# RWKV's triangular inverse by columns, experts' up projections in 512 + 512 + 384 columns, and a longer yield in the routing step

## The chip, the cores and the metric

The program runs on one core of a Trainium2 chip. The metric is the device time of one execution in microseconds (us). The engines are TensorE (PE; its weight loads are PEld), VectorE (DVE), ScalarE (ACT), GpSimd (POOL) and SyncE (SP, which here only starts loads).

## The reference

Two decoder layers over x of 512 tokens by 1024, in float32. Each layer mixes four branches of width 256 and then runs a feed-forward block, dense in the first layer and 2 of 8 experts in the second:

```
for l in range(2):
    h = rmsnorm(x)
    p_rw, p_sb, p_ret, p_conv = split(h @ w_in[l])          # 1024 -> 3328
    y = rwkv7(p_rw), stick_breaking(p_sb), retention(p_ret), conformer_conv(p_conv)
    x = x + (sum_i sigmoid(h @ w_gate[l, i]) * (y[i] @ w_branch[l, i])) @ w_out[l]
    h = rmsnorm(x)
    x = x + (swiglu(h, d_ff=2816) if l == 0 else top2_of_8_experts(h, d_ff=1408))

# rwkv7, per head: state = state * w + (state @ -kk) (x) (kk * a) + v (x) k ;  y = state @ r
# expert: (silu(h @ w1) * (h @ w3)) @ w2, gated by the softmax of the two chosen logits
```

## The kernel before

**Matmuls.** Activations lie with features on partitions and 512 tokens along the row. A product in full precision is three matmuls on a split of each operand into a high and a low part (`split`: ACT copies the high part, DVE subtracts to get the low one). In the mixers the weights come from DRAM through SP into `wraw`, and are split into `whi` and `wlo` of 512 columns; six split buffers of each run ahead of PE. Groups of 24 such matmuls (8 blocks of K, three passes; PSUM tag `mm`) form the weight stream of a layer: first the input projection in the order of `SEQ` (rwkv, retention, conv, stick-breaking), then per branch eight gate groups and eight branch groups, in the order retention, conv, rwkv, stick-breaking, then `w_out`.

**The order of the work.** The four mixers are Python generators that run beside the weight stream. The builder itself keeps a clock of each engine (`Clock`, with its own costs), and at each `slot()` between pieces of the stream it steps a generator when its results should be there (`pump`, `step`). `yield` means that the next step waits until the last is modelled to be finished; `yield NOW` lets it follow at the next slot; `yield 5000.0` waits 5000 ns more of the modelled PE time. So what each engine executes, and in what order, is fixed at build time by these costs; at run time every engine goes through its own list in order. All DVE, ACT and POOL instructions of helpers are recorded on line L213, matmuls on L473, transposes on L477, DMAs on L349, table loads on L370.

**RWKV's substitution.** RWKV works on 8 chunks of 64 tokens for 4 heads. Per chunk and head a unit lower triangular 64 x 64 matrix is inverted, as two 32 x 32 diagonal blocks and a product. All 64 diagonal blocks lie one to a partition: `L` is the strict triangle, `X` the inverse being made, `tmp` a buffer. Row t of X is the sum over earlier rows s of L[s, t] X[s]: one product over t x t elements, and one reduction over s, for t = 1 to 31. Afterwards X goes through DRAM (`d2`, `d3`, on POOL's queue) into `T11` and `TT`, and 32 x 32 matmuls form the rest.

**Stick-breaking chunks** (`sb_chunk`): scores on PE (`mx` buffers, three of them), a chain of exponentials, logarithms and scans on ACT and DVE, transposes back (L477), and a product into `po`.

**Experts.** Experts are sorted by load; ranks 0 to 3 have 192 rows, 4 to 7 have 128, and they run in the order 0, 4, 1, 5, ... The 64 overflow rows of the large ones cost two more matmuls per block (`po<-...`). Here the tokens are the stationary operand (`hh`, `hl`, and `ho` for overflow rows) and the weights stream: each unit of weights is loaded to `mraw`, split to `mhi` and `mlo`, and used. The up projections w1 and w3 go in column ranges `FQ`, the down projection in ranges of K, `FB`; `MRAW` and `MSPL` are the numbers of raw and split buffers. `turn` transposes a finished range of the hidden activations. `moe_prep` prepares the next expert: a one-hot table `O` (`moe_O`), slot tables and the gather (`moe_slots`), then, after `yield 20000.0`, transposes.

Of the kernel before, what the change touches and what calls it, by code (L numbers as in the profile page):

```python
# [19 lines left out]
KC = D // 128  # L20
# [10 lines left out]
N_IN = 3328  # L31
CAP = [192] * 4 + [128] * 4
NREST = 3
MRAW, MSPL = 6, 5
PORD = [0, 4, 1, 5, 2, 6, 3, 7]
NROW = S + 192
ARENA = 34
# [281 lines left out]
class Trunk:  # L319
# [188 lines left out]
    def rwkv(self, out):  # L508
# [154 lines left out]
        TT = m(Q, 64)  # L663
        g.memset(TT[:], 0.0)
        yield
        for t in range(1, 32):
            v.tensor_tensor(tmp[0:64, 0:t, 0:t], X[0:64, 0:t, 0:t].rearrange("p s c -> p c s"),
                            L[0:64, 0:t, t].unsqueeze(1).to_broadcast([64, t, t]), op=OP.mult)
            v.tensor_reduce(X[0:64, t, 0:t], tmp[0:64, 0:t, 0:t], axis=AX.X, op=OP.add)
            if t % 4 == 0 or t > 22:  # L670
                yield NOW
        L.free()
        v.tensor_copy(tmp[0:64], X[0:64].rearrange("p t c -> p c t"))
# [1076 lines left out]
                self.tr(ps[:, k - k0, :], src[0:m, k * 128:(k + 1) * 128], self.c("ident")[0:m, 0:m])  # L1750
            self.split(hi[:, k0:k1, :], lo[:, k0:k1, :], ps[:, 0:k1 - k0, :])

    FQ = [(0, 3), (3, 6), (6, 9), (9, 11)]
    FB = [(0, 3), (3, 6), (6, 9), (9, 11)]

    def moe_units(self, e):

        one = lambda w, a, b: w[bass.ds(e, 1), :, a:b].rearrange("o p f -> p (o f)")
        u = []
        for f0, f1 in self.FQ:  # L1760
            n = (f1 - f0) * 512
            for w in ("moe_w1", "moe_w3"):
                for o in (f0 * 1024, f0 * 1024 + n):
                    u.append((one(self.ins[w], o, o + n), n))
        for f0, f1 in self.FB:
            for d in range(2):
                o = d * (DFE // 128) * 512
                u.append((one(self.ins["moe_w2"], o + f0 * 512, o + f1 * 512), (f1 - f0) * 512))
        return u

    def m_load(self, n):
        while self.nld < min(n, len(self.units)):
            src, cols = self.units[self.nld]
            raw = self.wp.tile([128, 1536], F, name="mraw", tag="mraw", bufs=MRAW)
            self.turn(raw, "mraw", MRAW)
            self.load(raw[:, 0:cols], src, "sp")
            self.raws[self.nld] = raw
            self.nld += 1

    def m_split(self, n):  # L1780
        while self.nsp < min(n, len(self.units)):
            self.m_load(self.nsp + 1)
            cols = self.units[self.nsp][1]
            raw = self.raws.pop(self.nsp)
            t = [self.turn(self.wp.tile([128, 1536], R, name=x, tag=x, bufs=MSPL), x, MSPL) for x in ("mhi", "mlo")]
            self.split(t[0][:, 0:cols], t[1][:, 0:cols], raw[:, 0:cols])
            self.wts[self.nsp] = t
            self.nsp += 1
# [59 lines left out]
    def moe_prep(self, p, put):  # L1848

        slots = []  # L1850
        O = self.moe_O(self.moe_new, self.rkp[:, :, p], CAP[p])
        yield
        self.moe_slots(self.moe_new, O, self.V[:, :, p, :], CAP[p], slots)
        yield 20000.0
        H = [self.mt(n, [128, KC, 128], R, 2) for n in ("hh", "hl")]
        for k0 in (0, 4):
            self.moe_T(slots[0][2][:, k0 * 128:], 4, 128, H[0][:, k0:], H[1][:, k0:])
            yield
        if len(slots) > 1:
            o = self.mt("ho", [128, KC, 128], R, 2)  # L1860
            for k0 in (0, 4):
                self.moe_T(slots[1][2][:, k0 * 128:], 4, 64, o[:, k0:, 0:64], o[:, k0:, 64:128])
                yield
            H.append(o)
        put.append((slots, H))

    def moe_expert(self, slots, H, fill):
# [18 lines left out]
        def unit(blocks, ps, po, x, cols, first, last):  # L1886
            wt = self.m_weight()
            for i, k in enumerate(blocks):
                sl = slice(i * cols, (i + 1) * cols)
                self.stream(ps, po, (x[0][:, k, :], x[1][:, k, :]), x[2][:, k, :] if ov else None,  # L1890
                            (wt[0][:, sl], wt[1][:, sl]), first and i == 0, last and i == len(blocks) - 1)
                if i == 1 and len(blocks) > 2:
                    self.slot()

        for q, (f0, f1) in enumerate(self.FQ):
            n = (f1 - f0) * 128
            gm = self.mt("gm", [128, 384], bufs=2)[:, 0:n]
            go = self.mt("gmo", [64, 384], bufs=2)[:, 0:n] if ov else None
            for j in range(2):
                ps, po = self.ps("mm")[:, 0:n], self.ps("po")[:, 0:n] if ov else None  # L1900
                for h in range(2):
                    unit(range(4 * h, 4 * h + 4), ps, po, H, n, h == 0, h == 1)
                    if h == 0:
                        self.slot()

                def ev(j=j, ps=ps, po=po, gm=gm, go=go, n=n):
# [19 lines left out]
        for i, (f0, f1) in enumerate(self.FB):  # L1926
            for d, (ps, po) in enumerate(acc):
# [5 lines left out]
                            self.v.tensor_scalar(y[1][0:64, sl], self.fold(po, 512), w(1, 64), None, op0=OP.mult)  # L1933
                    self.pending.append(ev)
                self.slot()
                if d and i == 1:
                    for f in todo:
                        f()
                    todo.clear()
# [39 lines left out]
    def moe_rest(self):  # L1979
# [5 lines left out]
        def block(e, rk, V):  # L1985
# [8 lines left out]

            def weights():
                src, n = next(units)
                raw, hi, lo = tile_("rraw", [128, 1536]), tile_("rhi", [128, 1536], R), tile_("rlo", [128, 1536], R)
                nc.sync.dma_start(raw[:, 0:n], src)
                self.split(hi[:, 0:n], lo[:, 0:n], raw[:, 0:n])
                return hi, lo  # L2000
# [9 lines left out]
            for f0, f1 in self.FQ:  # L2010
                n, sl = (f1 - f0) * 128, slice(f0 * 128, f1 * 128)
                pr = [self.ps("mm")[:, 0:n] for _ in range(2)]
                for ps in pr:
                    for h in range(2):
                        unit(range(4 * h, 4 * h + 4), ps, x, n, h == 0, h == 1)
                self.a(gm[:, sl], pr[0], AF.Silu, scale=v[:, 2:3])
                self.v.scalar_tensor_tensor(gm[:, sl], pr[1], v[:, 2:3], gm[:, sl], op0=OP.mult, op1=OP.mult)
            self.moe_T(gm, nf, 128, g[0], g[1])
# [96 lines left out]
```

## Time and profile before

| | us |
|---|---|
| median of 3 runs (1970.99 to 1974.13) | 1971.04 |
| the profiled execution, its own time | 1968.11 |
| its span in the trace | 1966.2 |
| PE busy, share of the span | 1920.0 (98%) |
| DVE busy | 1310.9 (67%) |
| ACT busy | 975.9 (50%) |
| mixers of the first layer (to the dense block) | 8 to 405 |
| dense block | 405 to 920 |
| mixers of the second layer and output projection | 920 to 1405 |
| experts | 1426.7 to 1957.2 |

The stages follow each other in one execution. In the profile a row of the waits names who waited, who ended the wait, the total, the count and the longest. A row of the timeline gives start, duration, engine, line, operation, out<-in by the program's names, the shape and, in brackets, the idle time ahead of it. Durations of matmuls overlap, so their cost is read from one start to the next. A granted clock of 1.00 is TensorE at full speed.

### The profile page before, as it was taken

How to read it: one execution, taken by the hardware profiler on the slowest of the kernel's cores; microseconds unless marked ns; L12 is line 12 of the kernel's file. 1: busy time of each engine (PE TensorE's matmuls, PEld its weight loads, DVE VectorE, ACT ScalarE, POOL GpSimd, SP SyncE). 2: the span in 40 equal slices, each digit the busy share in tenths (PEclk: the TensorE clock that was granted, in tenths of full speed). 3: DMA queues.
4: the chain of work that ended last, by engine and by line, in shares of the span. 5: the costliest groups of instructions: out<-in, count | busy, mean ns of one | idle time of the engine just before them, and what ended most of it. 6: DMA issues, size and time to landing. Idle time of an engine off the chain costs nothing.

```text
span 1966.2 us, 26705 instructions
## 1 busy us (share of the span) xinstructions
PE 1920.0 (98%) x10172; PEld 1583.7 (81%) x10172; DVE 1310.9 (67%) x1970; ACT 975.9 (50%) x1429; POOL 123.7 (6%) x179
## 2 busy tenths in 40 slices
PE   8999899899999999999999999999999999999998
PEld 6778677688888888888778776778898998989987
DVE  6779986555653333356789976546477867768666
ACT  5643354743532232345453345644356756657665
POOL 1001100000000000000110100010101101001000
PEclk9999999999999999999999999999999999999999
DMA  5322311133333233243322322152377968969866
GB/s 190 104 76 76 99 59 64 59 118 99 99 108 97 97 97 97 91 131 125 97 65 81 94 68 71 59 166 92 137 268 246 361 215 293 331 216 330 280 220 215
DMA packets 74677, 284.54 MB, mean 145 GB/s; under 512 B 9536, under 2 KB 11200, under 8 KB 74544
## 3 DMA queue, kind: packets, MB, share of 16 engines
q1 hardware_dynamic: 65088, 254.04, 38.1%
q0 software_dynamic: 9312, 28.73, 5.3%
q8 instruction: 82, 1.34, 0.3%
q14 instruction: 51, 0.42, 0.1%
q10 hardware_dynamic: 144, 0.02, 0.0%
HBM read 266.23 MB, written 14.42 MB: 143 GB/s over the span
## 4 chain that ended last, share of the span: by engine, by line
PE 87%; DVE 6%; ACT 3%; issue 2%; DMA 1%; POOL 0%; SPq 0%; POOLq 0%; DVEq 0%; ACTq 0%
PE mm L473 67%; PE po L473 10%; PE mx L473 8%; DVE s L213 4%; ACT s L213 2%; PE mx L477 2%; DVE wlo L213 1%; DMA out_d<-y,si 1%; ACT whi L213 0%; DVE mlo L213 0%; DMA wraw<-w_gate_d 0%; DMA f<-xt_d 0%; ACT L370 0%; DVE uv L213 0%; ACT mhi L213 0%
## 5 line engine op out<-in xcount | busy, mean ns | idle before, releaser
L473 PE MATMUL mm<-s,whi 128*128 128x512 f32 x3168 | 1006.6, 399 | 20.7 <-DVE s L213 13.1
L473 PEld LDWEIGHTS mm<-s,whi 128*128 128x128 f32 x3168 | 591.2, 189 | 162.8 <-DVE s L213 18.1
L473 PE MATMUL mm<-s,wlo 128*128 128x512 f32 x1584 | 622.6, 393 | 2.2 <-DVE wlo L213 2.0
L213 ACT ACTIVATE whi<-wraw 128x512 fp32r<-128x512 f32 (+1 forms) x432 | 261.0, 620 | 243.4 <-PE mm L473 119.0
L213 DVE TENSOR_TENSOR wlo<-wraw,whi 128x512 fp32r<-128x512 f32 (+1 forms) x432 | 286.8, 680 | 124.2 <-ACT whi L213 123.3
L473 PEld LDWEIGHTS mm<-s,wlo 128*128 128x128 f32 x1584 | 299.8, 189 | 69.7 <-DVE wlo L213 5.9
L213 DVE TENSOR_TENSOR mlo<-mraw,mhi 128x1536 fp32r<-128x1536 f32 (+1 forms) x192 | 307.5, 1620 | 68.4 <-ACT mhi L213 67.8
L213 ACT ACTIVATE mhi<-mraw 128x1536 fp32r<-128x1536 f32 (+1 forms) x192 | 262.2, 1379 | 87.6 <-PE po L473 37.9
L213 DVE TENSOR_TENSOR s<-s,s 128x512 f32<-128x512 f32 (+15 forms) x306 | 222.2, 735 | 40.6 <-ACT s L213 32.5
L213 ACT ACTIVATE s<-s 128x512 f32<-128x512 f32 (+4 forms) x236 | 148.8, 658 | 187.8 <-DVE s L213 182.2
L473 PE MATMUL mm<-mhi,hh 128*128 128x384 f32 (+1 forms) x512 | 169.5, 331 | 0.0
L473 PE MATMUL mm<-mhi,hl 128*128 128x384 f32 (+1 forms) x512 | 165.5, 323 | 0.0
L473 PE MATMUL mm<-mlo,hh 128*128 128x384 f32 (+1 forms) x512 | 165.0, 322 | 0.3 <-DVE mlo L213 0.3
L213 ACT ACTIVATE s<-mm 128x512 f32<-128x512 f32 x108 | 64.1, 594 | 193.9 <-PE mm L473 193.9
L213 DVE TENSOR_TENSOR s<-s,mm 128x512 f32<-128x512 f32 x91 | 62.2, 685 | 136.4 <-PE mm L473 114.6
L473 PEld LDWEIGHTS mm<-mhi,hh 128*128 128x128 f32 x512 | 96.4, 188 | 2.3
L473 PEld LDWEIGHTS mm<-mlo,hh 128*128 128x128 f32 x512 | 96.4, 188 | 1.0 <-DVE mlo L213 1.0
L473 PEld LDWEIGHTS mm<-mhi,hl 128*128 128x128 f32 x512 | 96.5, 189 | 0.3
L473 PE MATMUL po<-mhi,ho 128*128 128x384 f32 (+1 forms) x256 | 83.3, 326 | 0.0
L473 PE MATMUL po<-mlo,ho 128*64 128x384 f32 (+1 forms) x256 | 82.3, 322 | 0.0
L213 DVE SCALAR_TENSOR_TENSOR s<-s,par,s 128x512 f32<-128x512 f32 (+31 forms) x110 | 77.4, 731 | 0.4
L473 PE MATMUL mm<-mhi,gh 128*128 128x512 f32 x176 | 70.5, 400 | 0.0
(180 smaller groups left out, 1871.6 us busy)
## 6 DMA issues: line engine op xcount, KB each, us to landing
mraw<-moe_w_d SPq DMA_DIRECT2D x144, 768.0 KB, 6.1
wraw<-w_gate_d SPq DMA_DIRECT2D x64, 512.0 KB, 3.5
wraw<-ffn_w_d SPq DMA_DIRECT2D x60, 512.0 KB, 3.5
wraw<-w_in_d SPq DMA_DIRECT2D x51, 512.0 KB, 3.5
mraw<-moe_w_d SPq DMA_DIRECT2D x48, 512.0 KB, 5.0
wraw<-w_branch_d SPq DMA_DIRECT2D x32, 256.0 KB, 2.7
wraw<-w_out_d SPq DMA_DIRECT2D x10, 512.0 KB, 3.8
wraw<-w_out_d SPq DMA_DIRECT2D x12, 256.0 KB, 2.8
```

Source lines behind the costliest of these rows:

```text
L213: return f(out, *a, **k)
L473: self.nc.tensor.matmul(out, lhsT, rhs, start=start, stop=stop)
L477: self.nc.tensor.transpose(out, in_, ident)
```

## The change

1. The substitution goes by columns: as soon as row s of X is done it is multiplied by its coefficients for all rows below, and the product is added to these rows. 31 products and 31 reductions of t x t elements become 31 products and 31 additions of (31 - s) x (s + 1) elements. It yields after every fourth step; before, it yielded after every fourth step up to 20 and then after each from 23.
2. The up projections go in 4 + 4 + 3 blocks of 128 columns, not 3 + 3 + 3 + 2, and in units of two blocks of K, 1024 columns at most (`KU`, `UNIT`), not four blocks and 1536 columns. The down projection goes in six ranges of K, not four. There are 9 raw and 7 split buffers of 1024 columns, not 6 and 5 of 1536. An expert has 36 units, not 24. The weights of w1 and w3 are laid out for it on the host.
3. `moe_prep` waits 5000 ns of modelled time after the one-hot table.

```diff
-    MRAW, MSPL = 6, 5
+    MRAW, MSPL = 9, 7
...
-        for t in range(1, 32):
-            v.tensor_tensor(tmp[0:64, 0:t, 0:t], X[0:64, 0:t, 0:t].rearrange("p s c -> p c s"),
-                            L[0:64, 0:t, t].unsqueeze(1).to_broadcast([64, t, t]), op=OP.mult)
-            v.tensor_reduce(X[0:64, t, 0:t], tmp[0:64, 0:t, 0:t], axis=AX.X, op=OP.add)
-            if t % 4 == 0 or t > 22:
+        for s in range(31):
+            sh = [64, 31 - s, s + 1]
+            v.tensor_tensor(tmp[0:64, s + 1:32, 0:s + 1], X[0:64, s, 0:s + 1].unsqueeze(1).to_broadcast(sh),
+                            L[0:64, s, s + 1:32].unsqueeze(2).to_broadcast(sh), op=OP.mult)
+            v.tensor_add(X[0:64, s + 1:32, 0:s + 1], X[0:64, s + 1:32, 0:s + 1], tmp[0:64, s + 1:32, 0:s + 1])
+            if s % 4 == 3:
                 yield NOW
...
-    FQ = [(0, 3), (3, 6), (6, 9), (9, 11)]
-    FB = [(0, 3), (3, 6), (6, 9), (9, 11)]
+    FQ = [(0, 4), (4, 8), (8, 11)]
+    FB = [(0, 2), (2, 4), (4, 6), (6, 8), (8, 10), (10, 11)]
+    KU = 2
+    UNIT = KU * 512
...
-            n = (f1 - f0) * 512
+            n = (f1 - f0) * 128 * self.KU
             for w in ("moe_w1", "moe_w3"):
-                for o in (f0 * 1024, f0 * 1024 + n):
+                for k in range(0, KC, self.KU):
+                    o = f0 * 1024 + k * (f1 - f0) * 128
                     u.append((one(self.ins[w], o, o + n), n))
...
         O = self.moe_O(self.moe_new, self.rkp[:, :, p], CAP[p])
-        yield
+        yield 5000.0
...
-                if i == 1 and len(blocks) > 2:
-                    self.slot()
...
-                for h in range(2):
-                    unit(range(4 * h, 4 * h + 4), ps, po, H, n, h == 0, h == 1)
-                    if h == 0:
+                for k in range(0, KC, self.KU):
+                    unit(range(k, k + self.KU), ps, po, H, n, k == 0, k + self.KU == KC)
+                    if k + self.KU < KC:
                         self.slot()
...
-                if d and i == 1:
+                if d and i == 2:
                     for f in todo:
                         f()
```

What it moves, at three places. First DVE in the first layer, at the end of the substitution (`s8` is tmp, `s25` is X, `s18` is L; the row that reads an `mm` buffer empties PSUM for the stream). Before:

```order
L213 TENSOR_TENSOR wlo_1841<-wraw_1744,whi_1840 128x512
L213 TENSOR_TENSOR s8_139<-s25_482,s18_335 64x30x30
L213 TENSOR_REDUCE s25_482<-s8_139 64x30
L213 TENSOR_TENSOR s33_630<-s13_168,mm_1861 128x512
L213 TENSOR_TENSOR wlo_1877<-wraw_1767,whi_1876 128x512
L213 TENSOR_TENSOR s8_139<-s25_482,s18_335 64x31x31
L213 TENSOR_REDUCE s25_482<-s8_139 64x31
L213 COPY s8_139<-s25_482 64x1024
```

After:

```order
L213 TENSOR_TENSOR s25_482<-s25_482,s8_139 64x31
L213 COPY s8_139<-s25_482 64x1024
L213 TENSOR_TENSOR s5_1798<-s19_340,s5_1798 128x512
L213 TENSOR_TENSOR s6_1801<-s27_527,s6_1801 128x512
L213 TENSOR_TENSOR wlo_1812<-wraw_1700,whi_1811 128x512
L213 TENSOR_TENSOR wlo_1828<-wraw_1700,whi_1827 128x512
L213 TENSOR_TENSOR wlo_1848<-wraw_1752,whi_1847 128x512
L213 TENSOR_TENSOR wlo_1864<-wraw_1752,whi_1863 128x512
L213 TENSOR_TENSOR s23_399<-s13_168,mm_1882 128x512
```

The substitution now ends four weight splits ahead of the first product that empties an `mm` buffer; before, two of its steps and the copy stood around that product. In all, eight other operations stand between its steps (nine in the second layer), before sixteen (seventeen).

Second, PE in the first layer: the second pair of heads' last two chunks. `s17` and `s30` are queries and keys; rows with `cst` are transposes. Before, with the scores of 256 columns:

```order
L477 MATMUL mx_3256<-cst_66,s11_153 128x128 x4
L473 MATMUL mx_3262<-s17_331,s30_601 128x256
L473 MATMUL mx_3263<-s17_331,s30_601 128x256
L473 MATMUL mm_3238<-s26_507,whi_3148 128x512 x2
L473 MATMUL mm_3238<-s26_507,wlo_3149 128x512
```

After:

```order
L473 MATMUL mm_3106<-s14_684,wlo_2999 128x512
L473 MATMUL mx_3162<-s17_331,s30_601 128x256
L473 MATMUL mx_3163<-s17_331,s30_601 128x256
L473 MATMUL mm_3178<-s22_389,whi_3023 128x512 x2
L473 MATMUL mm_3178<-s22_389,wlo_3024 128x512
```

These scores no longer stand directly behind another chunk's transposes; between them and their own transposes stand 48 matmuls of the stream, before 18. For the first pair of heads that distance is 12 now.

Third, PE at the start of the first expert (w1, overflow rows in `po`). Before:

```order
L473 MATMUL mm_11322<-mhi_11230,hh_11138 128x384
L473 MATMUL mm_11322<-mhi_11230,hl_11139 128x384
L473 MATMUL mm_11322<-mlo_11231,hh_11138 128x384
L473 MATMUL po_11323<-mhi_11230,ho_11140 128x384
L473 MATMUL po_11323<-mlo_11231,ho_11140 64x384
```

After:

```order
L473 MATMUL mm_11360<-mhi_11261,hh_11154 128x512
L473 MATMUL mm_11360<-mhi_11261,hl_11155 128x512
L473 MATMUL mm_11360<-mlo_11262,hh_11154 128x512
L473 MATMUL po_11361<-mhi_11261,ho_11156 128x512
L473 MATMUL po_11361<-mlo_11262,ho_11156 64x512
```

The same five matmuls per block of K now stream 512 columns, and a matmul of each kind is needed three times instead of four for all 1408 columns.

More of the change, by code (lines that the diff above doesn't have):

```diff
@@ L1773, in m_load @@
             src, cols = self.units[self.nld]
-            raw = self.wp.tile([128, 1536], F, name="mraw", tag="mraw", bufs=MRAW)
+            raw = self.wp.tile([128, self.UNIT], F, name="mraw", tag="mraw", bufs=MRAW)
             self.turn(raw, "mraw", MRAW)
@@ L1784, in m_split @@
             raw = self.raws.pop(self.nsp)
-            t = [self.turn(self.wp.tile([128, 1536], R, name=x, tag=x, bufs=MSPL), x, MSPL) for x in ("mhi", "mlo")]
+            t = [self.turn(self.wp.tile([128, self.UNIT], R, name=x, tag=x, bufs=MSPL), x, MSPL) for x in ("mhi", "mlo")]
             self.split(t[0][:, 0:cols], t[1][:, 0:cols], raw[:, 0:cols])
@@ L1891, in unit @@
                             (wt[0][:, sl], wt[1][:, sl]), first and i == 0, last and i == len(blocks) - 1)
-                if i == 1 and len(blocks) > 2:
-                    self.slot()
         for q, (f0, f1) in enumerate(self.FQ):
             n = (f1 - f0) * 128
-            gm = self.mt("gm", [128, 384], bufs=2)[:, 0:n]
-            go = self.mt("gmo", [64, 384], bufs=2)[:, 0:n] if ov else None
+            gm = self.mt("gm", [128, 512], bufs=2)[:, 0:n]
+            go = self.mt("gmo", [64, 512], bufs=2)[:, 0:n] if ov else None
             for j in range(2):
                 ps, po = self.ps("mm")[:, 0:n], self.ps("po")[:, 0:n] if ov else None
-                for h in range(2):
-                    unit(range(4 * h, 4 * h + 4), ps, po, H, n, h == 0, h == 1)
-                    if h == 0:
+                for k in range(0, KC, self.KU):
+                    unit(range(k, k + self.KU), ps, po, H, n, k == 0, k + self.KU == KC)
+                    if k + self.KU < KC:
                         self.slot()
@@ L1996, in weights @@
                 src, n = next(units)
-                raw, hi, lo = tile_("rraw", [128, 1536]), tile_("rhi", [128, 1536], R), tile_("rlo", [128, 1536], R)
+                raw, hi, lo = tile_("rraw", [128, self.UNIT]), tile_("rhi", [128, self.UNIT], R), tile_("rlo", [128, self.UNIT], R)
                 nc.sync.dma_start(raw[:, 0:n], src)
@@ L2013, in block @@
                 for ps in pr:
-                    for h in range(2):
-                        unit(range(4 * h, 4 * h + 4), ps, x, n, h == 0, h == 1)
+                    for k in range(0, KC, self.KU):
+                        unit(range(k, k + self.KU), ps, x, n, k == 0, k + self.KU == KC)
                 self.a(gm[:, sl], pr[0], AF.Silu, scale=v[:, 2:3])
```

## The prediction, made before the changed kernel ran

> **What bounds the kernel now.** I read the page's busy line first, then the stages, then who makes TensorE (PE) wait, then single rows in time.
>
> ```profile
> span 1966.2 us, 26705 instructions
> PE 1920.0 (98%) x10172; PEld 1583.7 (81%) x10172; DVE 1310.9 (67%) x1970; ACT 975.9 (50%) x1429; POOL 123.7 (6%) x179
> ```
>
> PE is busy for 98% of the span, so a gain is either less PE work or fewer of the 46 us in which it idles. By stages (start and end, length, then busy time and count of PE, weight loads, DVE, ACT and POOL, granted TensorE clock, share of the DMA engines, GB/s):
>
> ```profile
> 165.00:240.00 75.00, 67.43 (x290) 54.35 (x289) 73.02 (x119) 28.15 (x49) 5.04 (x9) 0.95 0.24 73
> 330.00:405.00 75.00, 67.46 (x384) 48.99 (x384) 49.43 (x79) 52.91 (x86) 0.00 (x0) 0.98 0.16 50
> 1190.00:1305.00 115.00, 105.53 (x581) 78.48 (x580) 66.89 (x107) 71.61 (x112) 4.86 (x8) 0.96 0.28 90
> 1426.70:1957.20 530.50, 530.10 (x3062) 479.87 (x3060) 397.29 (x411) 337.04 (x366) 41.59 (x22) 1.00 0.80 274
> ```
>
> In the experts (1426.7 to 1957.2) PE idles 0.4 us: there only less PE work counts. In the mixer stretches it idles 7 to 9 us each, and in the first of them VectorE (DVE) is busy 73 of 75 us and is the bound. PE's waits (total us, times, longest) in the windows 200 to 240, 1060 to 1100, 330 to 405 and 1190 to 1300:
>
> ```profile
> PE mm L473 <- DVE s L213: 6.3, 2, 5.8
> PE mm L473 <- DVE wlo L213: 1.3, 2, 0.7
> ...
> PE mm L473 <- DVE s L213: 3.1, 2, 2.0
> PE mm L473 <- DVE wlo L213: 0.7, 1, 0.7
> ...
> PE mx L473 <- ACT s L213: 3.5, 1, 3.5
> PE mx L477 <- ACT s L213: 3.3, 4, 1.4
> ...
> PE mx L473 <- ACT s L213: 5.2, 3, 3.6
> PE mm L473 <- DVE s L213: 3.0, 1, 3.0
> ```
>
> The first four rows, 11.4 us, fall on RWKV's two substitutions. The last four, 15.0 us, are the stick-breaking chunks and the end of RWKV. The longest wait in time:
>
> ```profile
> 226.53 1.08 DVE L213 TENSOR_REDUCE s<-s 64x30 f32<-64x900 f32 x1
> 227.64 0.69 DVE L213 TENSOR_TENSOR s<-s,mm 128x512 f32<-128x512 f32 x1
> ...
> 228.38 1.22 PE L473 MATMUL mm<-s,whi 128*128 128x512 f32 x2 [5.76 <-DVE s L213]
> ```
>
> The next group wants a PSUM buffer; the product that empties it (227.64) stands in DVE's order behind the last steps of the substitution. The wait has a second price, in the granted clock (the number before the DMA share) just after the long waits:
>
> ```profile
> 228.40:232.00 3.60, 3.60 (x9) 2.83 (x10) 3.53 (x4) 1.11 (x2) 0.00 (x0) 0.50 0.21 73
> 1098.70:1103.00 4.30, 4.29 (x12) 3.39 (x13) 4.30 (x7) 0.00 (x0) 1.32 (x2) 0.60 0.74 198
> 1299.00:1304.00 5.00, 5.00 (x13) 3.50 (x12) 0.72 (x2) 3.93 (x7) 0.00 (x0) 0.52 0.36 141
> ```
>
> Lost: 3.6 x 0.50 = 1.8, 4.3 x 0.40 = 1.7 and 5.0 x 0.48 = 2.4 us. The Trainium skill (TensorE: Matmul & The Clock Gate, on the clock gate) has the array fall to half clock after an idle window of about 3.4 us; here it fell after the second substitution's wait of 2.0 us too, so by that rule the 1.7 us would not be there, and the measurement decides.
>
> **The substitution.** Price of its instructions on DVE, first window 181.6 to 233.2 (busy, mean ns), then by shape:
>
> ```profile
> L213 DVE TENSOR_TENSOR s<-s,s 128x512 fp32r<-128x512 f32 (+31 forms) x33 | 25.3, 769 | 0.7
> L213 DVE TENSOR_REDUCE s<-s 64x1 f32<-64x1 f32 (+30 forms) x31 | 15.4, 495 | 1.1
> ...
> L213 DVE TENSOR_TENSOR s<-s,s 128x512 f32<-128x512 f32 x134 | 91.2, 689 | 14.6 <-ACT s L213 11.6
> L213 DVE TENSOR_TENSOR s<-s,s 64x961 f32<-64x961 f32 x2 | 3.8, 1922 | 0.0
> L213 DVE TENSOR_TENSOR s<-mx,cst 128x256 f32<-128x256 f32 x8 | 3.0, 415 | 4.3 <-PE mx L473 4.3
> ```
>
> Before: 25.3 less two operations of 512 that are not its own (1.4) is 23.9 us of products, plus 15.4 us of sums and 1.8 us of gaps: 41 us a layer. The product over 961 elements takes 2.0 ns an element; it reads both inputs in steps of 32. Operations on neighbouring elements cost (689 - 415) / 256 = 1.07 ns an element and 141 ns fixed. After: 62 operations, over (31 - s)(s + 1) elements, 5456 in all, once multiplied and once added: 62 x (0.141 + 0.03 gap) + 10912 x 1.07 ns = 10.6 + 11.7 = 22.3 us. DVE loses 18.7 us a layer. Should the broadcast product still cost 2.0 ns an element, it loses 13.6; both are more than the delay to be removed (the longest, 5.8 us), and nearly all of the steps lie ahead of that evacuation in DVE's order. So I take the waits of both substitutions (11.4 us) and the two slow-clock stretches behind them (1.8 + 1.7) as gone: -14.9. Bounds: -16, and -8 if half the waits come back as others.
>
> What is late next is the first matmul on the inverse (32x32), behind two trips through DRAM. In layer 0:
>
> ```profile
> 230.77 1.15 DVE L213 TENSOR_REDUCE s<-s 64x31 f32<-64x961 f32 x1
> ...
> 236.94 3.21 POOL L349 DMA_DIRECT2D s<-d  x5 [0.83 <-DMA d<-s]
> ...
> 246.13 2.11 PE L473 MATMUL mx<-s,f 32*32 32x32 f32 x64
> ```
> ```profile
> s<-d POOLq DMA_DIRECT2D x6, 64.0 KB, 2.9
> ```
>
> The last sum ended at 231.9, the last reload was issued at 240.15 and landed about 2.9 us later: data is ready 11 us after the last step. The new order puts this matmul 48 matmuls of the weight stream (11 us) earlier, and the waits taken away make it 9 us earlier still: 226. The chain ends 18.7 us earlier, and 5 more because eight instead of sixteen other operations of about 0.65 us stand between its steps: 208, ready at 219. That leaves 7 us; the same sum for layer 1 (66 matmuls, 15 us) leaves 5. New wait: 0, bounds 0 to +2. The first twelve steps now stand in one run of 24 operations, 8 us by the same prices; before, sixteen steps of 32 operations stood so, and PE did not wait there.
>
> **Stick-breaking chunks.** Nothing in them is edited, but their instructions fall elsewhere. Their waits are 15.0 us and the clock behind them (2.4 us at 1299, and two shorter ones). In layer 0 the last chunk's transposes move from 18 to 48 stream matmuls behind its scores, 11 us, which is enough for its dozen ACT and DVE operations (estimated 6 us, by the 415 and 689 ns of the rows above): the 3.5 us wait and its slow clock go. The first pair's third chunk now has 12 (2.7 us, some 4.5 with the other work there): a new wait of 2 to 3 us. In layer 1 the chunk behind the 3.6 us wait keeps its place. And the new order has 45 activation-table loads for 41, the four more all in layer 0's mixers, where (165 to 405) there are now:
>
> ```profile
> L370 ACT ACT_TABLE_LOAD x7 | 9.0, 1283 | 0.1
> ```
>
> Four more are 5 us on the engine that most of these waits name; ACT has 22 us free between 330 and 405, so some 2 us of it may be waited for. The three cancel: I take 0, with the bounds -18 (all waits and their clock gone) and +11 (two more long waits with their clock).
>
> **The experts.** Starts of matmuls by width (384, then 256, then 512):
>
> ```profile
> 1535.08 0.34 PE L473 MATMUL mm<-mhi,hh 128*128 128x384 f32 x1
> ...
> 1538.55 0.33 PE L473 MATMUL mm<-mlo,hh 128*128 128x384 f32 x1
> 1538.72 0.28 PE L473 MATMUL mm<-mhi,hh 128*128 128x256 f32 x1
> ...
> 1540.99 0.28 PE L473 MATMUL mm<-mhi,hl 128*128 128x256 f32 x1
> ```
> ```profile
> 1504.38 0.39 PE L473 MATMUL po<-mhi,go 128*128 128x512 f32 x1
> ...
> 1509.90 0.40 PE L473 MATMUL po<-mlo,go 128*64 128x512 f32 x1
> ```
>
> Twenty steps take 3.47 us (173.5 ns), 19 take 2.27 (119.5), 24 take 5.52 (230). Width 512 extended from the two narrower would be 227.5. Per block of K and pass, 3 x 173.5 + 119.5 = 640 ns becomes 2 x 230 + 173.5 = 633.5, or 628.5. There are 512 such (8 experts x 48, and 4 x 32 for overflow rows): -3.3 to -5.9, I take -4.6. The Trainium skill (TensorE: Matmul & The Clock Gate, on the 56 ns gap) gives a fixed cost of some 2.5 ns a matmul, with which 512 fewer matmuls save 1.3 us; the rows show about 11 ns (173.5 against 119.5 leaves 11.5 at width zero). Four groups of transposes per expert become three: 12 fewer breaks of the stream, -1 (estimated: a break costs less than one 256-wide step). The first unit's split is shorter, but its second is wanted sooner: 0. The yield of 5000 delays only the slot table of the next expert, which has 20000 more to wait by its own yield: 0, hidden by at least 50 us of expert.
>
> What grows is hidden: splits and loads come in 36 units instead of 24. The tightest window, an expert without overflow rows, and one with them:
>
> ```profile
> 1506.00:1559.50 53.50, 53.50 (x315) 49.15 (x314) 47.18 (x48) 40.10 (x41) 7.08 (x4) 1.00 0.95 334
> 1559.50:1639.00 79.50, 79.50 (x458) 71.35 (x457) 52.89 (x55) 45.08 (x52) 4.31 (x2) 1.00 0.73 245
> L213 DVE TENSOR_TENSOR mlo<-mraw,mhi 128x1536 fp32r<-128x1536 f32 x144 | 249.3, 1753 | 44.0 <-ACT mhi L213 43.6
> L213 DVE TENSOR_TENSOR mlo<-mraw,mhi 128x1024 fp32r<-128x1024 f32 x48 | 58.3, 1221 | 24.5 <-ACT mhi L213 24.2
> ```
>
> DVE's splits are 18 x 1.753 + 6 x 1.221 = 38.9 us an expert and become 26 x 1.221 + 8 x 0.96 + 2 x 0.69 = 40.8 (widths 768 and 512 by the slope): 49 of 53 us. SP issues half as many loads again, and it mostly waits for buffers. Experts: -5.6, say -5; bounds -8 to +6, the last from a rival below.
>
> **Sum.** -14.9 + 0 + 0 - 5 = -20. The profiled execution took 1968.1 us (span 1966.2) and the median of the runs is 1971.0, so I put the sum there: 1951. A difference under 0.2% (4 us) can't be told from none.
>
> **Rivals.** *Only the experts gain* (the planner's new order turns the substitution's waits into others of the same length): -5 and a few, 1965. For it: 15 us of waits sit where DVE is busy only 49 of 75 us. *The chunks' waits go too*: 11 to 18 us more, 1937; for it layer 0's longest wait, whose chunk is spread out, against it the table loads. *The DMA becomes the bound in the four lean experts*: the share is 0.95 already, in smaller pieces now. If those cost 10% of the rate, each of the four windows grows by 5% of 53.5, 2.7 us: +11, 1962. Against it: the experts with overflow rows that alternate with them leave a share of 0.73 (the second of those rows), and the buffered bytes are nearly the same (ten units of 1536 columns ahead, now fifteen of 1024). The Trainium skill (DMA: Bandwidth & Descriptors, measured bandwidth) asks for 1 MiB a transfer and gives 2 us fixed plus bytes at 436 GB/s; one transfer at a time that would be an estimated 112 us an expert against 88, but before's 66 us an expert already shows transfers overlapping. *Slower*: transposes placed close behind their scores make PE wait for ACT; one such wait costs 3.5 us and some 2 of slow clock. From four more of them than before the gain is spent; with five it ends at 1978. For it: the table loads, and the chunk that has only 12 matmuls.
>
> **Chances.** Forecast 0.55 (its own range 1943 to 1959); only the experts 0.16; chunks too 0.12; DMA 0.08; slower 0.09. Leaving out the slower case and the far ends of the others, the range is 1936 to 1967. Faster than 1967: 0.83 (a part of the second and the DMA case falls short); within 0.2%: 0.09; slower: 0.08.
>
> **What would show it.** Right: no wait of PE on DVE in the two substitution windows and a clock of 1.00 behind them; 62 DVE operations of 0.15 to 0.42 us; steps of about 230 ns in the up projections and an expert stage some 5 us shorter. Wrong: a wait at the 32x32 matmuls, PE waits for ACT at more chunk transposes, DMA at 0.99 with PE idle inside an expert.

## The result, and the profile after

The changed kernel takes 1926.59 us (median of 6 runs, 1925.36 to 1928.64), beside 1971.01 us for the kernel before in the same rounds. The ratio is 0.9773, with a 95% interval of 0.976 to 0.9785: 44.4 us less, where 20 were forecast with a range down to 1936. The profiled executions took 1968.11 us before and 1926.52 us after, 41.6 us less; the execution profiled before was 2.9 us shorter than the median of the runs there.

The head of the page after:

```profile
span 1924.7 us, 26363 instructions
PE 1900.6 (99%) x9660; PEld 1524.7 (79%) x9660; DVE 1279.2 (66%) x2034; ACT 990.1 (51%) x1499; POOL 120.0 (6%) x179
```

PE is still the bound, and its idle time has fallen from 46 to 24 us. By stages (columns as in the prediction), first before, then after. The cuts lie at the first matmul of the second layer on the weights `lora`, the last matmul of the weight stream and the first matmul of the experts, in both kernels:

```profile
0.00:935.19 935.19, 913.53 (x4498) 731.11 (x4498) 572.58 (x960) 402.88 (x675) 41.58 (x90) 0.99 0.31 99
935.19:1405.27 470.08, 456.60 (x2501) 353.54 (x2500) 329.87 (x550) 224.66 (x371) 36.75 (x63) 0.99 0.28 88
1405.27:1426.69 21.42, 19.73 (x116) 19.14 (x115) 11.15 (x51) 10.65 (x18) 2.25 (x3) 0.84 0.60 213
1426.69:1957.12 530.43, 530.11 (x3062) 479.88 (x3061) 397.30 (x411) 336.99 (x365) 41.59 (x22) 1.00 0.80 274
```
```profile
0.00:922.88 922.88, 910.93 (x4498) 729.00 (x4498) 554.26 (x960) 409.34 (x682) 42.33 (x90) 1.00 0.31 100
922.88:1373.63 450.75, 449.61 (x2501) 350.68 (x2500) 311.71 (x550) 223.82 (x370) 36.38 (x63) 1.00 0.29 92
1373.63:1392.01 18.38, 16.66 (x116) 15.85 (x115) 11.50 (x52) 9.91 (x18) 2.25 (x3) 1.00 0.57 193
1392.01:1915.66 523.65, 523.37 (x2550) 429.12 (x2549) 401.79 (x474) 346.29 (x429) 37.44 (x22) 1.00 0.82 279
```

The second number of a row is the stage's length: first layer -12.3 us, second layer's mixers and projections -19.3, routing -3.0, experts -6.8; together -41.4 of the span's -41.5. In the first two stages PE's busy time falls by 2.6 and 7.0 us, less than the lengths: most of what went is waits, the rest work at a slow clock. In the routing no wait went, and the granted clock rose from 0.84 to 1.00.

PE's waits in the whole of the changed kernel, the first five rows of that view (the 5.6 us are the kernel's first weights):

```profile
PE mm L473 <- ACT whi L213: 5.6, 1, 5.6
PE mm L473 <- DVE s L213: 3.2, 3, 2.4
PE mx L477 <- ACT s L213: 2.4, 4, 0.9
PE mx L473 <- ACT s L213: 1.0, 2, 0.8
PE mx L473 <- DVE uv L213: 0.9, 1, 0.9
```

Before, the second row had 13.1 us and the fourth 8.7. So not only the substitution's waits are gone, but nearly all long waits in the stick-breaking chunks too, in which nothing was edited.

The new substitution in the first layer (DVE: its group of operations from 181 to 210.1 us, one shape of it from 165 to 232 us, then its end and the first use of the inverse):

```profile
L213 DVE TENSOR_TENSOR s<-s,s 64x31 f32<-64x31 f32 (+16 forms) x63 | 21.4, 340 | 1.9
L213 DVE TENSOR_TENSOR s<-s,s 64x256 f32<-64x256 f32 x2 | 0.8, 416 | 0.1
```
```profile
208.90 1.11 DVE L213 COPY s<-s 64x1024 f32<-64x1024 f32 x1
...
224.74 2.11 PE L473 MATMUL mx<-s,f 32*32 32x32 f32 x64
```

One of the 63 operations, of 0.7 us, is not its own; that leaves 22.6 us with the gaps, 41 before. It ends at 208.9, and the 32x32 matmuls begin at 224.74 with no wait.

### The profile page after: what moved, and what is told of

The parts are those of the page before. It is cut to its first block, busy times and chain, and to the rows that moved or that the text cites. A ratio compares the mean times of both kernels' runs of the same rounds, so it can differ in the third digit from the quotient of the medians.

```text
span 1924.7 us, 26363 instructions
## 1 busy us (share of the span) xinstructions
PE 1900.6 (99%) x9660; PEld 1524.7 (79%) x9660; DVE 1279.2 (66%) x2034; ACT 990.1 (51%) x1499; POOL 120.0 (6%) x179
## 4 chain that ended last, share of the span: by engine, by line
PE 89%; ACT 4%; DVE 4%; issue 2%; DMA 1%; SPq 0%; POOL 0%; POOLq 0%; DVEq 0%; ACTq 0%
PE mm L473 69%; PE po L473 10%; PE mx L473 8%; ACT s L213 3%; DVE s L213 3%; PE mx L477 2%; DVE wlo L213 0%; ACT whi L213 0%; DMA out_d<-y,si 0%; ACT L370 0%; DMA f<-xt_d 0%; DVE mlo L213 0%; DVE uv L213 0%; ACT mhi L213 0%; SPq L349 0%
## 5 line engine op out<-in xcount | busy, mean ns | idle before, releaser
L213 DVE TENSOR_TENSOR mlo<-mraw,mhi 128x1024 fp32r<-128x1024 f32 (+2 forms) x288 | 317.4, 1130 | 78.7 <-ACT mhi L213 76.0
L213 ACT ACTIVATE mhi<-mraw 128x1024 fp32r<-128x1024 f32 (+2 forms) x288 | 277.6, 986 | 105.6 <-PE po L473 73.3
L213 ACT ACTIVATE s<-s 128x512 f32<-128x512 f32 (+3 forms) x238 | 150.0, 657 | 180.9 <-DVE s L213 178.8
L213 DVE TENSOR_TENSOR s<-s,s 128x512 f32<-128x512 f32 (+19 forms) x369 | 216.2, 593 | 37.4 <-ACT s L213 27.0
L473 PE MATMUL mm<-mhi,hh 128*128 128x512 f32 (+1 forms) x384 | 146.7, 382 | 0.0
L473 PE MATMUL mm<-mhi,hl 128*128 128x512 f32 (+1 forms) x384 | 143.3, 373 | 0.0
L473 PE MATMUL mm<-mlo,hh 128*128 128x512 f32 (+1 forms) x384 | 143.0, 372 | 0.3 <-DVE mlo L213 0.3
L473 PEld LDWEIGHTS mm<-mhi,hh 128*128 128x128 f32 x384 | 72.1, 188 | 12.3
L473 PE MATMUL po<-mlo,ho 128*64 128x512 f32 (+1 forms) x192 | 72.2, 376 | 0.0
L473 PE MATMUL po<-mhi,ho 128*128 128x512 f32 (+1 forms) x192 | 71.7, 374 | 0.0
```

The source lines that it names most:

```text
L213: return f(out, *a, **k)
L473: self.nc.tensor.matmul(out, lhsT, rhs, start=start, stop=stop)
```

## The experiments

All times are set against runs of the kernel before on the same chip. Stage lengths are those of the profiled execution, cut as above. The lengths of a stage differ somewhat between runs in which PE executes the same order: before, experts alone and yield 5000 alone have 470.1 to 474.8 us in the second layer, and after, after again, substitution alone, plain yield and old widths have 921.5 to 923.9 us in the first.

| run | first layer | second layer | routing | experts | median | ratio, 95% |
|---|---|---|---|---|---|---|
| before | 935.19 | 470.08 | 21.42 | 530.43 | 1969.4 to 1971.4 | 1 |
| after | 922.88 | 450.75 | 18.38 | 523.65 | 1926.59 | 0.976 to 0.9785 |
| substitution alone | 921.52 | 450.69 | 18.37 | 530.42 | 1933.65 | 0.9803 to 0.9835 |
| experts alone | 935.19 | 474.78 | 18.37 | 530.73 | 1971.57 | 1.0 to 1.0023 |
| new arithmetic, old order | 927.31 | 464.69 | 21.17 | 530.43 | 1954.42 | 0.9905 to 0.9938 |
| old arithmetic, new order | 939.17 | 464.67 | 18.37 | 530.50 | 1966.98 | 0.9973 to 0.9994 |
| yield 5000 alone | 936.36 | 470.93 | 21.19 | 530.45 | 1970.10 | 0.999 to 1.0009 |
| after, plain yield | 923.62 | 450.75 | 18.38 | 531.69 | 1937.59 | 0.9816 to 0.9852 |
| after, old widths | 921.83 | 452.36 | 21.06 | 535.95 | 1939.88 | 0.9823 to 0.9856 |
| true price | 931.46 | 468.67 | 21.12 | 530.42 | 1962.37 | 0.9935 to 0.9968 |
| after again | 923.87 | 450.67 | 18.37 | 523.64 | 1927.45 | 0.9774 to 0.981 |
| after, old yields | 926.32 | 450.75 | 21.41 | 523.65 | 1932.48 | 0.9793 to 0.9828 |
| after, yield 8 | 928.79 | 451.95 | 21.43 | 523.64 | 1935.21 | 0.9809 to 0.9844 |
| after, scan price | 919.22 | 452.54 | 21.11 | 523.66 | 1925.66 | 0.976 to 0.9795 |
| old price, new yields | 922.38 | 460.40 | 18.38 | 530.62 | 1942.94 | 0.9838 to 0.9871 |
| long price | 924.41 | 465.11 | 21.42 | 530.41 | 1952.12 | 0.9882 to 0.9915 |
| old order, no fill | 927.44 | 464.93 | 18.38 | 530.48 | 1952.71 | 0.9893 to 0.9926 |

### The two halves of the change

**The substitution alone**, on the kernel before:

```diff
-        for t in range(1, 32):        # products and reductions by rows
...
+        for s in range(31):           # products and additions by columns, as in the change
...
+            if s % 4 == 3:
                 yield NOW
```

> Before with the new substitution alone. The mixers of both layers came out 31.6 us shorter in the changed kernel and the routing stage 3.0 us, the experts 6.8 us. If the substitution (its work and the order it brings) makes all of the mixers' part, this gives 1971 - 31.6 = 1939, or 1936 with the routing stage's 3.0; all 10 waits of the before kernel in the mixers, 3 us long and more, are gone. My prediction's account (only the waits at the substitutions and the clock behind them) gives 1956.

1933.65: the substitution brings 37 us. The layers take what they take in the changed kernel.

**The experts alone**, on the kernel before: widths, units, buffers and the place of `todo`.

```diff
-MRAW, MSPL = 6, 5
+MRAW, MSPL = 9, 7
...
-    FQ = [(0, 3), (3, 6), (6, 9), (9, 11)]
+    FQ = [(0, 4), (4, 8), (8, 11)]
...
+    KU = 2
...
```

> Before with the new widths, units and buffers of the experts alone; substitution and yield as before. If the experts' stage gains the same by itself: 6.8 us shorter, 1964, with the mixers' waits as before (3.6 us and 3.0 us at 1190 to 1305 among them). If the stage gained only because the mixers no longer delay its first loads: under 2 us, 1969 or more.

The numbers of the second, but not its reason: 1971.57, and the experts' stage takes 530.73 us. PE waits now, where it did not before, at the first use of the one-hot table `O` in three of seven experts, and that has eaten the gain:

```profile
PE mx L473 <- DVE O L213: 5.8, 3, 1.9
```

### Work or order

**New arithmetic in the old order.** The builder's clock is charged for the old operations, and the new ones are issued past it:

```diff
+            self.clock.run("dve", cost, [tmp[0:64, 0:t, 0:t]], [X..., L...])     # old price, old operands
+            self.clock.run("dve", cost, [X[0:64, t, 0:t]], [tmp[0:64, 0:t, 0:t]])
+            v.eng.tensor_tensor(tmp[0:64, s + 1:32, 0:s + 1], ...)               # new operations
+            v.eng.tensor_add(X[0:64, s + 1:32, 0:s + 1], ...)
             if t % 4 == 0 or t > 22:
                 yield NOW
```

> Before with the new products and additions, but in exactly the old order on every engine: the builder's clock is given the old prices, operands and yields, so only the 62 DVE instructions of each substitution differ. Work theory (DVE has less to do, and that makes the gain): the waits at the substitutions go, and those 100 us behind them too: 1937 to 1940. Order theory (the waits of the stick-breaking chunks belong to the order, which is unchanged): only the substitutions' 11.4 us of waits and 3.5 us of slow clock go, and the 15 us of waits in the chunks stay: 1956.

1954.42, 16 us less. Every engine executes the old order. The waits at the substitutions are gone, and those of the chunks stay, the longest one grown from 3.6 to 5.4 us (rows of PE's waits in the second layer, 1180 to 1400):

```profile
PE mx L473 <- ACT s L213: 7.1, 3, 5.4
PE mm L473 <- DVE s L213: 3.0, 1, 3.0
PE mm L473 <- ACT whi L213: 1.3, 1, 1.3
```

**Old arithmetic in the new order**: the same device the other way round, on the kernel with the substitution alone. PE, ACT and POOL execute the order of the changed kernel's mixers.

> The other half: the old products and reductions in the order of the kernel with the new substitution alone; only the 62 DVE instructions of each substitution differ from that one. They take some 41 us of DVE a layer where the order has room for 22, so DVE runs up to 19 us late. Work theory: the chunk waits come back with the lateness, 1971 or more. Order theory: the waits at 1190 to 1305 stay away (13.7 us with their clock) and only the substitutions' own waits are there, longer than before by a few us: 1957 to 1966.

1966.98, just above the order theory's window. The waits for DVE grew to 26.4 us, some 22 of them at the substitutions (up to 7 us), and the chunks' waits for ACT stayed away, though DVE now runs late:

```profile
PE mm L473 <- DVE wlo L213: 17.1, 5, 6.8
PE mm L473 <- DVE s L213: 9.3, 3, 6.2
...
PE mx L473 <- ACT s L213: 0.8, 1, 0.8
```

So two effects are told apart: less work on DVE takes away the substitution's own waits, and the order takes away the chunks'. Alone they bring 16 and 4 us, together 37: with the old arithmetic, the new order pays at the substitutions what it saves at the chunks.

**The true price**: before, with the clock charged for what the old product really takes.

```diff
+            self.t["dve"] += 76.0 + 0.81 * t * t
             v.tensor_reduce(X[0:64, t, 0:t], tmp[0:64, 0:t, 0:t], axis=AX.X, op=OP.add)
```

> Before, arithmetic of the substitution unchanged, but the builder's clock is charged 76 + 0.81 n ns more for each product of n elements, about what the trace shows above its price (1887 ns for 961 elements, where it reckons 1070), so that the order is laid out for the real durations. Theory (the waits come from an order laid out too tightly): the wait of 5.8 us and the ones near it go without a faster substitution, 1942 to 1956. Rival (DVE is busy 73 of 75 us there, and no order hides 41 us of work): waits of PE for DVE of 8 us or more remain at the substitutions, 1962 or more.

1962.37, the rival's time, and with 7.5 us nearly its waits: the wait for DVE of 5.8 us is gone, but ones of 2.3, 3.8 and 1.4 us stand at the substitutions, and behind the second one there are new ones, of 5.0 us for ACT and 3.5 for DVE. In the whole of that run:

```profile
PE mm L473 <- ACT s L213: 7.8, 3, 5.0
PE mm L473 <- DVE s L213: 7.6, 4, 3.5
...
PE mm L473 <- DVE wlo L213: 3.8, 1, 3.8
```

### Is each order a draw?

**The changed kernel again**, for the chip:

> The changed kernel as it is, on this chip, as the measure for the three that follow: 1925 to 1929 by its first runs. The experiment without the longer yield came out 11 us above the changed kernel's first runs, where its profile shows 8.0 us in the experts' stage; if this one is at 1929 here, the rest was the chip.

1927.45, within that range.

**Old yields**, **a yield every eight steps**, and **the scans' price** in the builder, each on the changed kernel:

```diff
-            if s % 4 == 3:
+            if s % 4 == 3 or s > 21:     # old yields
```
```diff
-            if s % 4 == 3:
+            if s % 8 == 7:               # every eight steps
```
```diff
+        if name == "tensor_tensor_scan":
+            return 69.0 + 2.11 * n       # else 69.0 + 1.042 * n
```

> The changed kernel, but the substitution yields as the old one did: after every fourth step and after each step from the 23rd on. The arithmetic is unchanged; the order of the mixers on all engines becomes another one. Theory (the 22 us that the new order brought are one draw among orders: the builder lays the stick-breaking chunks out anew each time, sometimes with waits): waits of 1.4 to 3.5 us at the chunks come back in part, 5 to 15 us with their clock, 1931 to 1941. Rival (with a short substitution any order has few waits): 1929 or less.

> The changed kernel with a yield after every eighth step of the substitution, another draw: up to 16 operations of DVE in a row, some 6 us. Theory (the order is a draw): a time that differs from the changed kernel by several us, 1929 to 1941, by waits far from the substitution. Rival (any order with a short substitution is good): within 3 us of the changed kernel.

> The changed kernel, but the builder's clock is told what the trace shows for the scans of the stick-breaking chunks: 1211 ns for 512 elements (69 + 2.11 n), where it reckons 602. If the waits at the chunks come from this wrong price, the 6 us of waits that are left in the mixers (the longest 2.4 us) fall to 2 or less: 1921 to 1924. If the order is a draw and the price does not matter: the time differs by several us, more likely longer, 1927 to 1940.

1932.48, 1935.21 and 1925.66. The draw theory is half right at most. The first two profiles are 5.5 and 8.9 us longer than that of the changed kernel again, but 3.0 us of each are the routing's clock (last section), and 2.4 and 4.9 us the first layer. There the orders differ by up to 9.6 us (919.22 to 928.79), by single waits such as one of 3.1 us at a chunk with the old yields and one of 4.5 us with a yield every eight steps; one order alone differs by 2.4. In the second layer all four orders lie within 450.7 to 452.5. The scan's price gives the best first layer, but 1.8 us beside 1927.45 is no more than the runs of one kernel differ; nothing here is shown to be faster than the changed kernel.

**Old price with new yields, and a long price**, both on the kernel with the new arithmetic in the old order:

```diff
-            if t % 4 == 0 or t > 22:
+            if t % 4 == 0:                            # old price, new yields
```
```diff
+            self.t["dve"] += 76.0 + 0.81 * t * t      # long price
```

> Before with the new arithmetic and the new yields (every fourth step), while the builder reckons with the old price of the substitution (26.0 us). The second layer's mixers and output projection take 464.7 us with old price and old yields, 450.8 with new price and old yields, 450.7 with both new. If the price makes it: about 464 here, chunk waits of 3 us and more in the second layer, 1950 or more. If the yields alone suffice too, or each order is a draw: 451 to 458, 1934 to 1944.

> Before with the new arithmetic in exactly the order of the experiment with the true price (the builder reckons with 36.8 us; only the 62 DVE instructions of each substitution differ from it). There the second layer took 468.7 us, with waits of 5.0 and 3.5 us for ACT and DVE behind the substitution. If these waits belong to the order: both are here too, the 3.8 us wait on the weight split at the substitution is gone, second layer 462 to 467, 1948 to 1957. If they came from DVE's lateness: 451 to 455, 1936 to 1942.

1942.94 (second layer 460.40, between the two forecasts) and 1952.12 (465.11). In the second run the waits of 5.0 and 3.5 us are there again, though DVE has less to do: they belong to the order. With the new arithmetic throughout, orders laid out for a substitution of 15.6 us (and in one case dearer scans) have a second layer of 450.7 to 452.5, orders laid out for 26.0 or 36.8 us one of 460.4 to 465.1, whatever the yields. Seven orders are few, but the two groups don't overlap. Whether the yields bring a part (460.4 against 464.7) is not shown, since one order differs by as much between runs. Which of the builder's rules turns the short price into the better order was not tried.

### One wait followed to its head

The longest wait in the second layer before is named as one for ACT. Its chain (ACT, then POOL, then PE, before):

```profile
1288.24 2.18 ACT L213 ACTIVATE whi<-wraw 128x512 fp32r<-128x512 f32 x4
1296.79 0.63 ACT L213 ACTIVATE whi<-wraw 128x512 fp32r<-128x512 f32 x1 [6.37 <-DMA wraw<-w_gate_d]
1297.33 0.58 ACT L213 ACTIVATE s<-mm 128x512 f32<-128x512 f32 x1
1297.80 1.24 ACT L213 ACTIVATE s<-mx 128x512 f32<-128x512 f32 x3
```
```profile
1289.43 1.08 POOL L349 DMA_DIRECT2D xd<-s  x2 [0.30 <-POOL s L213]
1290.51 1.13 POOL L349 DMA_DIRECT2D out_d<-s  x2
```
```profile
1298.44 1.22 PE L473 MATMUL mx<-s 64*128 64x256 f32 x2 [3.56 <-ACT s L213]
```

The scores want an `mx` buffer. The copy that empties it (1297.80) stands on ACT behind a weight split (1296.79), which waits 6.37 us for its load, and at that time POOL's queue fills rows of `xd` and `out_d` with zeros for the routing. In the changed kernel the same pieces stand so:

```profile
1267.50 0.63 ACT L213 ACTIVATE whi<-wraw 128x512 fp32r<-128x512 f32 x1 [4.03 <-DMA wraw<-w_gate_d]
1268.04 0.58 ACT L213 ACTIVATE s<-mm 128x512 f32<-128x512 f32 x1
1268.62 1.09 ACT L213 ACTIVATE s<-mx 128x512 f32<-128x512 f32 x2
```
```profile
1268.22 0.96 POOL L213 MEMSET s<- 128x1024 f32 x1 [5.81 <-ACT whi L213]
1269.47 1.08 POOL L349 DMA_DIRECT2D xd<-s  x2 [0.30 <-POOL s L213]
```
```profile
1268.95 1.02 PE L473 MATMUL mx<-s 64*128 64x256 f32 x4
```

The fills start after the load has landed, ACT's wait is shorter, and PE comes later and does not wait. To test this, the fill of `out_d` (rows that are not returned) is left out of the old order with the new arithmetic, and nothing else:

```diff
+                self.clock.run("pool", 1040.0, ..., "ring", ...)     # still reckoned with
+                if dst is self.xd:
+                    self.nc.gpsimd.dma_start(d, s)
```

> The new arithmetic in the old order again, but the zeros for the output's rows behind the 512 tokens (two transfers, 768 KB together, on POOL's queue) are left out; the builder still reckons with them, and all else on every engine is in the same order. If the traffic delays the weight load, ACT's wait for it (8.2 us) falls by 2.1 to 2.8 us (768 KB at the 279 to 366 GB/s of these rows), PE's wait of 5.4 us falls as much, and the time by 2 to 4 us: 1950.5 to 1952.5. If ACT's own chain makes the wait: the wait stays at 5 us and the time at 1954.

PE's row at that place, with the fill and without:

```profile
1285.81 1.22 PE L473 MATMUL mx<-s 64*128 64x256 f32 x2 [5.41 <-ACT s L213]
```
```profile
1283.50 1.22 PE L473 MATMUL mx<-s 64*128 64x256 f32 x2 [2.91 <-ACT s L213]
```

ACT's wait fell from 8.22 to 5.74 us and PE's by 2.50, as the traffic theory says. So this fill makes nearly half of the wait; what makes the other 2.9 us was not separated. The time does not show the gain: 1952.71 and, on another chip, 1954.42 have overlapping intervals, and of the 2.3 us between the two profiles nothing is left beside the routing's clock (18.38 us against 21.17). The stage is no shorter. The granted clock is 0.89 and 0.69 in two windows of 4 us from 1372, where it was 1.00 with the fill: 1.7 us. And the half clock behind the wait ends near 1289.6 us in both, so that PE, which starts 2.3 us earlier, spends these at half speed.

The other long wait there is of the same kind on DVE. A product that empties PSUM at 1208.09 stood behind ACT's sigmoid, which stood behind a chunk's operations and a table load (ACT, then DVE, before):

```profile
1206.13 1.28 ACT L370 ACT_TABLE_LOAD   x1
1207.43 1.67 ACT L213 ACTIVATE s<-s 128x512 f32<-128x512 f32 x3
```
```profile
1208.09 0.69 DVE L213 TENSOR_TENSOR s<-s,mm 128x512 f32<-128x512 f32 x1 [4.60 <-ACT s L213]
```

### The experts

**The longer yield alone**, on the kernel before:

```diff
-        yield
+        yield 5000.0
         self.moe_slots(self.moe_new, O, self.V[:, :, p, :], CAP[p], slots)
```

The run has the same line in `moe_first` too, where it does nothing: the builder steps that generator by hand and leaves its yields unread.

> Before with the longer yield alone. In the kernel before, 14 to 26 matmuls stand on PE between the start of the table O on DVE and its first use, and no use waits. Theory (the yield is needed only with the smaller units): nothing to win, 1969 to 1973. Rival (it moves work in the experts so that the stage is shorter by itself): the experts' stage under 528 us, 1968 or less.

1970.10: nothing, as said.

**The changed kernel with the plain yield**, the line in `moe_prep` the other way round:

> The changed kernel with the plain yield after the table O. In the run of the experts' edit alone, three times no matmul of the stream stood between O and its first use, and PE waited 5.8 us for it. Theory (smaller units make more slots, so that the next step of the routing comes at once; the yield holds it back): the three waits are here too, the experts' stage about 530 us, 1932 to 1933. Rival (those waits came from the old substitution's order of loads): no wait for O, 1926 to 1928.

1937.59: beside 1927.45 on the same chip the yield is worth 10 us, 8.0 of them in the experts' stage of the profile. The waits for `O` are there, 5.8 us again, and the last is followed by a slow stretch (clock 0.72: 6.0 x 0.28 = 1.7 us):

```profile
1797.47 1.03 PE L473 MATMUL mx<-V,O 128*128 128x4 f32 x8 [1.94 <-DVE O L213]
```
```profile
1797.50:1803.50 6.00, 6.00 (x24) 4.69 (x25) 0.44 (x2) 1.06 (x1) 0.00 (x0) 0.72 0.96 294
```

The rest was not the chip. In the four runs the granted clock goes with the time: 0.997 at 1934.51 and 1935.60, 0.994 at 1939.57 and 1940.59. The theory's reason does not hold, though: by the code an expert has 36 points at which another generator can step in (`slot()`), and 46 before. Why a plain yield lets the table and its first use meet only with the new units stays open.

**The changed kernel with the old widths**:

```diff
-    FQ = [(0, 4), (4, 8), (8, 11)]
+    FQ = [(0, 3), (3, 6), (6, 9), (9, 11)]
```

> The changed kernel with the up projections in 384 + 384 + 384 + 256 columns again, the units still of two blocks of K, with the new buffers, down projection and yield. Theory (the stage's 6.8 us come from the widths, 512 matmuls fewer at about 12 ns each and a group of transposes fewer): stage about 530 us, 1933. Rival (the units and the down projection bring part of it): stage 526 us or less, 1929 or less. Second rival (units of 768 and 512 columns are too small): over 532 us, 1936 or more.

1939.88, the second rival: the stage takes 535.95 us, 5.5 more than with the old units. 3.1 us of it are new waits of PE for the folding and the hidden activations:

```profile
PE po L473 <- DVE fold L213: 2.4, 4, 0.8
...
PE mm L473 <- DVE gl L213: 0.4, 2, 0.2
PE mx L477 <- DVE gm L213: 0.3, 1, 0.3
```

Another 7.4 us stand in the starts of the up projections' matmuls (336.3 us in sum, 328.8 in the changed kernel); the rest was not separated. So the stage's 6.8 us are a difference of larger things: with the small units the widths save 12.3 us and the yield 8.0, and without either the units would cost.

## Why the prediction was wrong

It failed on one term: **"The three cancel: I take 0"** for the stick-breaking chunks. By stages the forecast and the result are:

| term | forecast | shown | by |
|---|---|---|---|
| substitution's waits and clock | -14.9 (-16 to -8) | -13.3 | first two stages, new arithmetic in the old order less before |
| chunks | 0 (-18 to +11) | -18.4 | the same stages, after less that run |
| routing | none | -3.0 | granted clock |
| experts | -5 (-8 to +6) | -6.8 | stage lengths |

By medians the steps from before to the new arithmetic, to the substitution alone and to the changed kernel are -16.2, -20.8 (with the routing) and -7.1 us.

**Substitution: right.** 22.3 us of DVE forecast, 22.6 measured; its end at 208 forecast, 208.9 measured; the 32x32 matmuls at 226 and without a wait, 224.74 and none. The broadcast product and the addition in place take 416 ns for 256 elements, as neighbouring elements do.

**Chunks: wrong, by the whole term.** The step that failed is the offset: the waits that go in layer 0 were set against new ones there, and layer 1's were kept. Shown is -18.4 us, 4.4 in the first layer and 13.9 in the second: from the new arithmetic in the old order to the changed kernel PE's idle time in the two falls by 12.8 us, and its busy time, with the same matmuls at a higher clock, by 5.6. The estimate counted matmuls between a chunk's scores and its transposes, and kept the 3.6 us wait because "the chunk behind the 3.6 us wait keeps its place". But at the head of that wait stood a weight load beside POOL's fills, and the fills moved; with the new arithmetic in the old order, where it lasts 5.4 us, one fill makes 2.5 of them. For the other waits that went, only that they go with the order is shown. The table loads did grow by four (ACT is 6.5 us busier in the first layer), and no long wait for ACT came of it; the 2 to 3 us wait forecast for the first pair's third chunk is not seen (the longest at any chunk's transposes is 0.9 us), but a new one of 2.4 us, for DVE, ends at 334. The rival in which the chunks' waits go too, priced at 1937 and given 0.12, is what happened, at the far end of its 11 to 18 us.

**Routing: missing.** The half clock after the routing's two short waits was in the trace of before (0.84 above), and was not counted, since those waits of 0.8 and 0.9 us stay. They stayed, and the clock did not fall. That is luck, not a gain of the change: in runs with the same order on PE up to there it falls in one and not in another (before 21.42 us and experts alone 18.37; after 18.38 and old widths 21.06).

**Experts: mechanism right, three sizes off.** The up projections' starts, summed over the trace, fell from 335.3 to 328.8 us, -6.5 for -4.6. The mean pitches over all of them are 178.0 ns (384, before), 120.9 (256) and 232.5 (512), not the 173.5, 119.5 and 230 of the rows chosen; the first pass of each block of K is the dearest (183.3 ns at 384, the next two 177.4 and 174.8). The yield at "0, hidden by at least 50 us of expert" was true only beside the old units. The claim that the units' own changes cost nothing was wrong too: without the longer yield they cost all that the widths gain. That these two errors cancelled is luck.

**Rivals.** DMA did not become the bound: the experts' share went from 0.80 to 0.82, and PE idles 0.3 us in them. The 2 us a transfer of the prediction's last estimate there is stated by the Trainium skill (DMA: Bandwidth & Descriptors, Anatomy of one DMA) for transfers issued from GpSimd; the experts' weights are issued by SP, and no run here shows what one costs alone. A slower kernel by new chunk waits: none longer than 2.4 us.

## What to carry to other kernels

Where a builder lays out the order by its own prices, a cheaper step is two changes: less work, and a new order everywhere behind it. The first can be read from the trace; for the second, take the sum of all waits and slow clock in what is laid out anew as a possible gain, not as an unlikely end, since nearly half of this kernel's gain was there. Follow each wait past the engine that the profile names, through what stands ahead in that engine's order, to the load or table at its head: only then can one say whether it "keeps its place". And a new division of the stream can bring a table and its first use together, as in three of seven experts here: look for what then stands between them.

## What the hardware showed that was not expected

The same 116 matmuls of the routing, with the same waits of 0.8 and 0.9 us, ran at half clock for some 7 us in 9 of the 17 profiles (21.1 to 21.4 us) and at full clock in 8 (18.4). Before, then after:

```profile
1409.30:1416.90 7.60, 7.57 (x35) 7.60 (x36) 3.52 (x12) 2.77 (x5) 2.25 (x3) 0.55 0.40 130
```
```profile
1377.60:1384.00 6.40, 6.28 (x48) 6.10 (x48) 3.44 (x12) 2.86 (x6) 2.25 (x3) 1.00 0.46 164
```

The wait of 2.4 us that ends at 334 was followed by a clock of 0.63 from 336 to 340 in the changed kernel and of 1.00 with the substitution alone. And with old price and new yields the clock fell with no wait of PE at all, behind matmuls of 8 columns:

```profile
1364.69 0.96 PE L473 MATMUL po<-rt,f 128*128 128x8 f32 x8
1365.51 1.05 PE L477 MATMUL mx<-cst,f 128*128 128x128 f32 x4
```
```profile
1365.50:1368.50 3.00, 3.00 (x12) 2.51 (x12) 1.38 (x2) 0.60 (x1) 2.99 (x5) 0.51 0.80 247
```

So the price of a wait's clock is 0 or some 1.5 to 3 us here (4.0 x 0.37 = 1.5 in the changed kernel, 3.0 in the routing), and what decides was not tried. The Trainium skill (TensorE: Matmul & The Clock Gate, Part 1) has the gate watch activity over a free-running window, so that the same program can fall on either side; the routing's two lengths agree with that, but no run here shows the window itself.
